# Units' lower parts are emitted one product later, and each MLP begins with a group of direct tiles, second-product tiles and 14 units

## The chip, the core and the metric

The kernel runs on one core of a Trainium2 chip. The core has five engines that run side by side and wait for each other through semaphores: TensorE (PE) multiplies matrices, VectorE (DVE), ScalarE (ACT) and GpSimd (POOL) work element by element, and SyncE (SP) issues the DMAs that bring weights from HBM. The on-chip memories are SBUF (operands) and PSUM (where TensorE accumulates). The metric is the device time of one launch in microseconds.

## The reference, cut to what matters

A trunk of two layers over 528 tokens (16 learned ones and 512 of the input), model width 1024. Layer 0 mixes with retention and gated DeltaNet heads, layer 1 with a Mamba-2 mixer. Each mixer is followed by a layernorm and by an MLP, and it is the two MLPs that the change touches:

```python
def sq_relu_mlp(h, w1, w2):
    return jnp.square(jax.nn.relu(h @ w1)) @ w2

for i in range(DEPTH):
    ...
    h = layer_norm(DN_ALPHA * h + mix, ln1_w[i], ln1_b[i])
    h = layer_norm(DN_ALPHA * h + sq_relu_mlp(h, mlp_w1[i], mlp_w2[i]), ln2_w[i], ln2_b[i])
return h[:, N_META:]
```

`w1` is 1024 x 4096 and `w2` 4096 x 1024, all in float32.

## The kernel before

**Precision.** A float32 product is made of three matmuls on split operands: high times high, high times low, low times high (`mm3`, L176 to L178). Every operand is therefore split once: ScalarE casts it to the high part (L152), VectorE subtracts to get the low part (L153). `halve` does this to a 1024-wide weight block, whose tiles are named `w`; activations split so are named `s`, and `hh` and `hl` are the halves of the normalised input of the MLP.

**Shape of the MLP.** `mlp()` is called for layer 0 and for layer 1. The tokens stand in the matmul's columns, in two halves: 272 and 256 in layer 0, 256 and 256 in layer 1, which drops the 16 learned tokens. Half a unit's columns are `nh`, 264 or 256. The hidden width of 4096 is 8 groups of 4 tiles of 128. A tile of the first product is 8 steps of 3 matmuls; in layer 1 some products run over 512 columns at once.

**Direct tiles.** `phase` (L191) runs tiles of the first product one after the other. The result is read from PSUM by `evac_u` (L445): ScalarE takes the Relu (L451), GpSimd squares it (L453), ScalarE squares it again into the rounded high part (L459), and VectorE subtracts the high part from GpSimd's square to get the low part (L460). High and low part are then the operands of the second product.

**Units.** From the second half of group 1 on, tiles come in pairs (`Unit`), as a Strassen-Winograd product: tiles i and i + 2 of a group, both halves of their rows and both halves of the tokens, in seven products of 12 matmuls (L514) instead of eight. `prepare` loads the weights, forms the sums s1 to s4 of weight quarters on VectorE (L487 s1, L488 s3, L490 s2, L491 s4) and splits all of them. `combos` makes the matching differences of the input (L408). `run` takes the products in the order a11, s1, s2, a12, s3, s4, a22. Three PSUM banks are used: `ba` for a11, s2, s3 and at last a22, `bb` for a12, `bc_` for s1 and s4. ScalarE copies intermediate sums out (L518, L521, L524) into the three rows x1, x2, x3, and VectorE adds to them: x1 += `bb` (L527), x2 += `ba` (L531), x3 += `bc_` (L535). The a22 product goes on writing into `ba`, so it has to wait until L531 has read it. Each of x1, x2, x3 and the final `ba` goes through `evac_u`.

**Second product.** `Four` takes four output tiles of `w2` for one group (96 matmuls in layer 0, 48 of 512 columns in layer 1) and adds them to the residual (`accumulate`: L385 the first time, L383 afterwards). It reads the high and low parts of all four tiles of its group.

**What sets the order.** The program is written as a list of `stages`; while one stage runs, `adv()` is called after each of its products and moves the preparation of the next stage on by one step, and `tick()` does the same for other spawned work such as `combos`. A scheduler fixes the order of the instructions of each engine when the kernel is built. Each engine then runs its instructions strictly in that order: an instruction that waits holds up everything behind it on its engine. Before the change, an MLP runs group 0 and tiles 0 and 2 of group 1 directly, then `unit(1, 1)`, `four(0, 0)`, `four(0, 1)`, and then in turn a unit of group c and a `Four` of group c - 1: 13 units per MLP.

Of the kernel before, what the change touches and what calls it, by code (L numbers as in the profile page):

```python
# [12 lines left out]
F32 = mybir.dt.float32  # L13
# [3 lines left out]
ADD, SUB, MUL, MIN, MAX, POW = ALU.add, ALU.subtract, ALU.mult, ALU.min, ALU.max, ALU.pow  # L17
# [40 lines left out]
def trunk(ctx: ExitStack, tc: tile.TileContext, a, out):  # L58
    nc = tc.nc
    V, G, S, T, SY = nc.vector, nc.gpsimd, nc.scalar, nc.tensor, nc.sync  # L60
# [37 lines left out]
    def spawn(gen):  # L98
        tasks.append(gen)
        return gen  # L100
# [18 lines left out]
    def wait(cond):  # L119
        while not cond():  # L120
            yield

    def until(cond):
        while not cond():
            tick()
# [14 lines left out]
    def pause(n):  # L140
        for _ in range(n):
            yield
# [29 lines left out]
    def wload(src, n=1024, raw=None):  # L172
        return halve(fetch(src, n) if raw is None else raw, n)
# [17 lines left out]
    def phase(tiles, rhs, evac, ns, head=0, tail=0, ready=None):  # L191

        def both(blks, key):
            o = pm(512)
            product(o, blks, rhs[2], every=4)
            for hf in range(2):
                evac(key, hf, o[:, hf * 256:hf * 256 + 256])
            tick()  # L200

        def run(hf, blks, key, m=P):
            o = pm(ns[hf], part=m)
            product(o, blks, rhs[hf], m=m)
            evac(key, hf, o)
            tick()
        n = len(tiles)
        for i0, i1 in [(0, head)] + [(i, i + 1) for i in range(head, n - tail)] + [(n - tail, n)]:
            held = []
            for srcs, *key in tiles[i0:i1]:  # L210
                held.append(([b for s in srcs for b in (s if isinstance(s, list) else s() if callable(s) else wload(s))], *key))
                if len(rhs) > 2 and head <= i0 < n - tail:
                    both(*held.pop())
                    continue
                if ready is not None and i0 == 0:
                    until(lambda: ready(0))
                run(0, *held[-1])
            if ready is not None and i0 == 0:
                until(lambda: ready(1))
            for args in held:  # L220
                run(1, *args)
# [20 lines left out]
    hx = [htile() for _ in range(KT)]  # L242
# [148 lines left out]
    def combos(h, ns, nh, go, get):  # L391

        def quarter(k, c):

            a, b = h[0][k], h[1][k]
            if c == 0:
                return [(0, nh, a[:, 0:nh])]
            cut = ns[0] - nh
            return ([(0, cut, a[:, nh:ns[0]])] if cut else []) + [(cut, nh, b)]

        def diff(out, x, y):
            if not isinstance(y, list):
                y = [(0, nh, y)]
            for o, e, ap in x:
                for o2, e2, ap2 in y:
                    lo, hi = max(o, o2), min(e, e2)
                    if lo < hi:
                        V.tensor_tensor(out[:, lo:hi], ap[:, lo - o:hi - o], ap2[:, lo - o2:hi - o2], op=SUB)  # L408

        yield from wait(go)  # L410
        for k in range(4):
            q0, q1 = [[quarter(i, c) for c in range(2)] for i in (k, k + 4)]
            d = [tl("m", nh) for _ in range(4)]
            diff(d[0], q0[1], q0[0])
            diff(d[2], q1[1], q0[1])
            diff(d[1], q1[1], d[0])
            diff(d[3], q1[0], d[1])
            for j in range(4):
                get(j, k, d[j])
                if j % 2:  # L420
                    yield

    def mlp(l, hx, h, ns, ready, evac0, pairs, final=None):
# [3 lines left out]
        w1, w2 = a["mw1"], a["mw2"]  # L427
        nh = (ns[0] + ns[1]) // 2
        NG, GF = 8, 4
        tt = [[None] * 4 for _ in range(4)]  # L430
# [7 lines left out]
        def half(k, i):  # L438
            return tuple(x[:, i * nh:(i + 1) * nh] for x in pairs[k])

        def group():
            u = [[None] * GF for _ in hx]
            us = [None] * GF

            def evac_u(f, hf, o, n=None):  # L445
                if n is None:
                    n, off = ns[hf], hf * ns[0]
                else:
                    off = hf * n
                t = tl("m", n)  # L450
                S.activation(t, o, AF.Relu)  # L451
                q = tl("m", n)
                G.tensor_tensor(q, t, t, op=MUL)  # L453
                if us[f] is None:
                    us[f] = pair = tl("s", L, F32R), tl("s", L, F32R)
                    for dst, x in zip(u, parts(pair, ((0, ns[0]), (ns[0], ns[1]), (0, 512)))):
                        dst[f] = x
                hi, lo = [x[:, off:off + n] for x in us[f]]
                S.activation(hi, t, AF.Square)  # L459
                V.tensor_tensor(lo, q, hi.bitcast(F32), op=SUB)  # L460
            return u, evac_u

        def second_src(c, m):
# [123 lines left out]

        groups = [group() for _ in range(NG)]

        def unit(c, i):  # L590
            return Unit(c, i, lambda f, hf, o: groups[c][1](f, hf, o, nh))

        def four(c, i):
            return Four(c, groups[c][0], 4 * i)

        stages = [unit(1, 1), four(0, 0), four(0, 1)]
        for c in range(2, NG):
            stages += [unit(c, 0), four(c - 1, 0), unit(c, 1), four(c - 1, 1)]
        last = [four(NG - 1, 0), four(NG - 1, 1)] if final is None else [Rows()]
        gens = [st.gen for st in stages + last]  # L600
        spawn(combos(h, ns, nh, lambda: ready(1), get))
        ahead = []

        def third():
# [3 lines left out]

        phase([([w1[l, 0]], 0), ([w1[l, 1]], 1), ([third], 2), ([lambda: halve(ahead[0])], 3)], hx, groups[0][1], ns,
              head=3, ready=ready)  # L610
        spawn(gens[0])

        def second():
            blks = wload(w1[l, GF + 2])
            next(gens[1])
            return blks

        phase([([w1[l, GF]], 0), ([second], 2)], hx, groups[1][1], ns)
        until(lambda: "s4" in stages[0].ops and all(x is not None for y in tt for x in y))
        B += [[half(k, 0) for k in range(4)], [half(k, 0) for k in range(4, 8)],  # L620
              [half(k, 1) for k in range(4, 8)], tt[3], tt[0], tt[1], tt[2]]
        for i, st in enumerate(stages):
            if i + 2 < len(gens):
                next(gens[i + 2])

            def adv():
                next(gens[i + 1], None)
                tick()
            st.run(adv)
            for _ in gens[i + 1]:  # L630
                pass
        for _ in gens[-1]:
            pass
        if final is not None:
            final(groups[-1][0][2], last[0].blks, h)
            return
        blks = last[0].blks + last[1].blks
# [511 lines left out]
    y = [[None] * 16, [None] * 16]  # L1149
# [21 lines left out]
    hn, hp, ready = norm_after(r, ns0, PP_LN, PP_LN + 8)  # L1171
# [3 lines left out]
    hn, hx, ready1 = norm_after(r, ns0, PP_LN + 16, PP_LN + 24)  # L1175
# [203 lines left out]
    for g in range(4):  # L1379
        f = []  # L1380
# [20 lines left out]
    for m in range(3):  # L1401
        blks = wload(srcs[m][0]) + wload(srcs[m][1][:, 0:512], 512)
        o = pm(512)
# [173 lines left out]
```

## Time and profile before

| | us |
|---|---|
| median of three runs | 1718.58 |
| the three runs | 1712.72, 1718.58, 1718.89 |
| profiled execution, its time | 1710.59 |
| profiled execution, its span in the trace | 1708.8 |
| busy: PE, DVE, ACT, POOL | 1662.7, 1154.1, 739.0, 316.9 |

The span is the time that the trace covers; the 1.8 us beside it lie around it. The mean granted clock of TensorE is 0.994 of full speed. PE is counted busy in 97% of the span, but matmuls are pipelined and their ends are modelled, so the start of one matmul to the start of the next is the better measure. The units of layer 0 run between about 575 and 872 us of the span, those of layer 1 between about 1380 and 1665 us. In a row of the trace the line is that of the kernel's text, tile names stand without their numbers, and `pmm` and `pmx` are PSUM tiles.

### The profile page before, as it was taken

The page shows a single profiled execution, that of the slowest core. Times are in us where ns is not written, and L with a number is a line of the kernel's source. Part 1 is how long each engine was busy: PE and PEld are TensorE (multiplying, and loading weights), DVE is VectorE, ACT ScalarE, POOL GpSimd, SP SyncE. Part 2 cuts the span into 40 slices and gives each one's busy share as a digit, 9 for nine tenths or more (in the row PEclk, how much of TensorE's full clock was granted, in tenths as well). Part 3 has the DMA queues.
Part 4 walks back from the last instruction along what each step waited for, and adds up shares of the span by engine and source line. Part 5 has one row for each costly group of instructions (what it writes and reads, how often), then busy time and mean ns, then how long its engine had stood idle before and what let it go on. Part 6 is the DMA issues. An engine that isn't in the chain of part 4 may idle for free.

```text
span 1708.8 us, 29912 instructions
## 1 busy us (share of the span) xinstructions
PE 1662.7 (97%) x11884; PEld 1529.0 (89%) x11884; DVE 1154.1 (68%) x2300; ACT 739.0 (43%) x1509; POOL 316.9 (19%) x360
## 2 busy tenths in 40 slices
PE   9899999999999999999999999999999999999998
PEld 7898998899999999999998988888778888888886
DVE  5896667666437857766657776858553876666665
ACT  4432245554214534444434665656432544444441
POOL 1211210010003301111102034242410321111112
PEclk9999999999999999999999999999999999999999
DMA  6233212112222322222221443333222222222231
GB/s 219 83 95 93 70 38 69 50 51 79 95 75 69 106 93 96 81 97 99 88 71 63 139 117 110 108 111 112 68 86 96 79 99 93 98 94 96 92 116 49
DMA packets 88484, 155.60 MB, mean 91 GB/s; under 512 B 11864, under 2 KB 43224, under 8 KB 88344
## 3 DMA queue, kind: packets, MB, share of 16 engines
q1 hardware_dynamic: 88200, 153.53, 28.1%
q8 instruction: 93, 1.52, 0.4%
q14 instruction: 47, 0.39, 0.1%
q10 hardware_dynamic: 144, 0.16, 0.0%
HBM read 148.92 MB, written 4.75 MB: 90 GB/s over the span
## 4 chain that ended last, share of the span: by engine, by line
PE 81%; DVE 8%; ACT 3%; POOL 3%; issue 2%; DMA 2%; SPq 0%; POOLq 0%; DVEq 0%; ACTq 0%
PE pmm L178 19%; PE pmm L177 19%; PE pmm L176 19%; PE pmm L514 7%; PE pmx L514 4%; POOL m L453 2%; ACT w L152 1%; DVE w L153 1%; PE pmx L1439 1%; DVE s L650 1%; DMA w<-in_w 1%; PE pmx L1289 1%; ACT m L451 1%; DVE s L460 1%; PE pmx L1293 1%
## 5 line engine op out<-in xcount | busy, mean ns | idle before, releaser
L176 PE MATMUL pmm<-hh,w 128*128 128x256 f32 (+5 forms) x1480 | 455.2, 308 | 5.6 <-ACT s L643 2.0
L178 PE MATMUL pmm<-hh,w 128*128 128x256 f32 (+3 forms) x1480 | 443.4, 300 | 0.2 <-DVE w L153 0.2
L177 PE MATMUL pmm<-hl,w 128*128 128x256 f32 (+3 forms) x1480 | 442.0, 299 | 1.2 <-DVE hl L344 0.9
L153 DVE TENSOR_TENSOR w<-w,w 128x1024 fp32r<-128x1024 f32 (+2 forms) x253 | 312.3, 1236 | 147.7 <-PE pmm L177 79.8
L152 ACT CAST w<-w 128x1024 fp32r<-128x1024 f32 (+2 forms) x253 | 260.9, 1032 | 347.5 <-PE pmm L177 88.9
L176 PE MATMUL pmm<-s,w 128*128 128x256 f32 (+2 forms) x1136 | 361.2, 318 | 0.0
L178 PE MATMUL pmm<-s,w 128*128 128x256 f32 (+2 forms) x1136 | 360.8, 318 | 0.0
L177 PE MATMUL pmm<-s,w 128*128 128x256 f32 (+2 forms) x1136 | 360.3, 317 | 0.0
L176 PEld LDWEIGHTS pmm<-hh,w 128*128 128x128 f32 (+2 forms) x1480 | 279.0, 189 | 19.5 <-issue 4.2
L177 PEld LDWEIGHTS pmm<-hl,w 128*128 128x128 f32 (+1 forms) x1480 | 278.8, 188 | 12.5 <-issue 2.1
L178 PEld LDWEIGHTS pmm<-hh,w 128*128 128x128 f32 (+1 forms) x1480 | 279.0, 189 | 8.8 <-DVE w L153 0.7
L177 PEld LDWEIGHTS pmm<-s,w 128*128 128x128 f32 x1136 | 213.7, 188 | 14.3 <-DVE s L1368 0.3
L176 PEld LDWEIGHTS pmm<-s,w 128*128 128x128 f32 x1136 | 213.9, 188 | 14.0
L178 PEld LDWEIGHTS pmm<-s,w 128*128 128x128 f32 x1136 | 213.7, 188 | 14.1
L453 POOL TENSOR_TENSOR m<-m 128x256 f32<-128x256 f32 (+2 forms) x128 | 117.1, 917 | 534.3 <-ACT m L451 530.8
L147 POOL TENSOR_TENSOR n<-n,neg 128x1 f32<-128x1 f32 (+2 forms) x58 | 40.3, 699 | 439.3 <-DVE n L146 418.7
L650 DVE SCALAR_TENSOR_TENSOR s<-s,pp,s 128x528 f32<-128x528 f32 x120 | 102.2, 851 | 27.1 <-ACT s L648 24.9
L383 DVE TENSOR_TENSOR m<-m,pmm 128x272 f32<-128x272 f32 (+1 forms) x208 | 81.7, 415 | 19.1 <-PE pmm L178 19.0
L460 DVE TENSOR_TENSOR s<-m,s 128x256 fp32r<-128x256 f32 (+2 forms) x128 | 64.9, 508 | 43.9 <-POOL m L453 41.5
L514 PE MATMUL pmm<-s,s 128*128 128x264 f32 (+1 forms) x624 | 83.8, 283 | 0.1
L514 PEld LDWEIGHTS pmm<-s,s 128*128 128x128 f32 x624 | 78.5, 188 | 0.5 <-DVE s L153 0.3
L527 DVE TENSOR_TENSOR row<-row,pmx 128x264 f32<-128x264 f32 (+1 forms) x26 | 11.0, 424 | 97.2 <-PE pmx L514 97.2
(313 smaller groups left out, 2464.8 us busy)
## 6 DMA issues: line engine op xcount, KB each, us to landing
w<-in_w SPq DMA_DIRECT2D x88, 512.0 KB, 3.2
w<-in_mw SPq DMA_DIRECT2D x146, 256.0 KB, 3.1
w<-in_mw SPq DMA_DIRECT2D x38, 512.0 KB, 3.3
w<-in_wo SPq DMA_DIRECT2D x29, 512.0 KB, 3.3
row<-rd SPq DMA_DIRECT2D x16, 512.0 KB, 5.6
sp<-in_mw SPq DMA_DIRECT2D x26, 256.0 KB, 2.7
s<-rd SPq DMA_DIRECT2D x32, 128.0 KB, 5.8
w<-in_w2n SPq DMA_DIRECT2D x4, 512.0 KB, 3.2
```

What stands on the lines that cost most here:

```text
L147: G.tensor_tensor(dst, t, neg5[0:part, 0:n], op=POW)
L152: S.copy(dst_hi, src)
L153: V.tensor_tensor(dst_lo, src, dst_hi.bitcast(F32), op=SUB)
L176: T.matmul(o, w[0], x[0], start=first, stop=False)
L177: T.matmul(o, w[0], x[1], start=False, stop=False)
L178: T.matmul(o, w[1], x[0], start=False, stop=last)
L383: V.tensor_tensor(t, t, o, op=ADD)
L451: S.activation(t, o, AF.Relu)
L453: G.tensor_tensor(q, t, t, op=MUL)
L460: V.tensor_tensor(lo, q, hi.bitcast(F32), op=SUB)
L514: T.matmul(o, w[x][:, c], B[b][k][y], start=first and k == i == 0, stop=last and k == 3 and i == 2, skip_group_check=True)
L650: V.scalar_tensor_tensor(acc, cin[:, k:k + L], w[k], acc, op0=MUL, op1=ADD)
```

## The change

Two things are done in `mlp()`.

First, the subtraction that makes the low part (L460) is no longer emitted in `evac_u` when a unit calls it. It is put on the list `late`, and `lower()`, called at the beginning of each `adv()`, emits those that were listed one product earlier. (In the changed file these subtractions have the line L598, those of direct tiles L462; a unit's additions are L531, L535 and L539 for L527, L531 and L535, its matmuls L518 for L514, and L487 to L491 become L491 to L495.)

Second, tiles 0 and 2 of group 1 are no longer direct tiles. Behind group 0 comes at once `four(0, 0)`, then `unit(1, 0)`, `four(0, 1)`, `unit(1, 1)`, and then the old sequence: 14 units per MLP. The weights of `four(0, 0)` are loaded and split during group 0 (`begin`), and `combos` starts one step later.

```diff
@@ combos
         yield from wait(go)
+        yield
         for k in range(4):
@@ group
-            def evac_u(f, hf, o, n=None):
+            def evac_u(f, hf, o, n=None, late=None):
...
                 S.activation(hi, t, AF.Square)
-                V.tensor_tensor(lo, q, hi.bitcast(F32), op=SUB)
+                if late is None:
+                    V.tensor_tensor(lo, q, hi.bitcast(F32), op=SUB)
+                else:
+                    late[-1].append((lo, q, hi.bitcast(F32)))
@@ mlp
+        late = [[], []]
+
+        def lower():
+            for lo, q, hi in late.pop(0):
+                V.tensor_tensor(lo, q, hi, op=SUB)
+            late.append([])
+
         def unit(c, i):
-            return Unit(c, i, lambda f, hf, o: groups[c][1](f, hf, o, nh))
+            return Unit(c, i, lambda f, hf, o: groups[c][1](f, hf, o, nh, late))
...
-        stages = [unit(1, 1), four(0, 0), four(0, 1)]
+        def begin():
+            yield from wait(lambda: ready(1))
+            yield from pause(2)
+            yield from gens[0]
+
+        stages = [four(0, 0), unit(1, 0), four(0, 1), unit(1, 1)]
         for c in range(2, NG):
             stages += [unit(c, 0), four(c - 1, 0), unit(c, 1), four(c - 1, 1)]
...
         spawn(combos(h, ns, nh, lambda: ready(1), get))
+        spawn(begin())
...
-        spawn(gens[0])
-
-        def second():
-            blks = wload(w1[l, GF + 2])
-            next(gens[1])
-            return blks
-
-        phase([([w1[l, GF]], 0), ([second], 2)], hx, groups[1][1], ns)
-        until(lambda: "s4" in stages[0].ops and all(x is not None for y in tt for x in y))
+
+        until(lambda: len(stages[0].blks) == 4 and all(x is not None for y in tt for x in y))
...
+        next(gens[1])
         for i, st in enumerate(stages):
             if i + 2 < len(gens):
                 next(gens[i + 2])
 
             def adv():
+                lower()
                 next(gens[i + 1], None)
                 tick()
             st.run(adv)
...
         for _ in gens[-1]:
             pass
+        lower()
+        lower()
```

VectorE around the additions of one unit in the middle of layer 0's MLP, before. The `row` tile holds x1, x2 and x3; `w` 128x1024 is a weight block being split, `s` 128x264 a low part:

```order
L527 TENSOR_TENSOR row_7822<-row_7822,pmx_7820 128x264
L153 TENSOR_TENSOR w_8003<-w_7813,w_8002 128x1024
L460 TENSOR_TENSOR s_7888<-m_7885,s_7887 128x264
L531 TENSOR_TENSOR row_7822<-row_7822,pmm_7819 128x264
L535 TENSOR_TENSOR row_7822<-row_7822,pmx_7821 128x264
L460 TENSOR_TENSOR s_7909<-m_7906,s_7908 128x264
```

and in the changed kernel, around the same unit:

```order
L531 TENSOR_TENSOR row_7835<-row_7835,pmx_7833 128x264
L153 TENSOR_TENSOR w_8016<-w_7826,w_8015 128x1024
L535 TENSOR_TENSOR row_7835<-row_7835,pmm_7832 128x264
L539 TENSOR_TENSOR row_7835<-row_7835,pmx_7834 128x264
L598 TENSOR_TENSOR s_7901<-m_7898,s_7900 128x264
L598 TENSOR_TENSOR s_7921<-m_7918,s_7920 128x264
```

The low part has left its place between the weight block and the x2 addition; now it stands behind the x3 addition, and the weight block is directly ahead of the x2 addition.

TensorE at the end of the same unit before, where `pmx` with `hh` is the last of product s4, `pmm` with 128x272 the following `Four` and `pmm` with 128x264 the product a22:

```order
L514 MATMUL pmx_7821<-hl_6448,s_7795 128x264
L514 MATMUL pmx_7821<-hh_6447,s_7796 128x264
L176 MATMUL pmm_7955<-s_6987,w_7836 128x272
L514 MATMUL pmm_7819<-s_6678,w_7741 128x264 x2
L514 MATMUL pmm_7819<-s_6678,w_7742 128x264
```

and in the changed kernel:

```order
L518 MATMUL pmx_7834<-hl_6448,s_7808 128x264
L518 MATMUL pmx_7834<-hh_6447,s_7809 128x264
L518 MATMUL pmm_7832<-s_6719,w_7754 128x264 x2
L518 MATMUL pmm_7832<-s_6719,w_7755 128x264
L518 MATMUL pmm_7832<-s_6814,w_7754 128x264 x2
```

The first matmul of the `Four` no longer stands ahead of a22.

VectorE ahead of the first unit's additions in layer 0, before, with the preparation of the next unit (L487, L488, L490) between them:

```order
L460 TENSOR_TENSOR s_7073<-m_7105,s_7072 128x256
L153 TENSOR_TENSOR s_7126<-s_7028,s_7125 128x512
L487 TENSOR_TENSOR w_7267<-sp_7268,w_7267 128x512
L527 TENSOR_TENSOR row_7138<-row_7138,pmx_7136 128x264
L488 TENSOR_TENSOR sp_7268<-w_7265,sp_7268 128x512
L153 TENSOR_TENSOR w_7286<-w_7129,w_7285 128x1024
L460 TENSOR_TENSOR s_7204<-m_7201,s_7203 128x264
L531 TENSOR_TENSOR row_7138<-row_7138,pmm_7135 128x264
L490 TENSOR_TENSOR sp_7268<-w_7267,w_7265 128x512
L535 TENSOR_TENSOR row_7138<-row_7138,pmx_7137 128x264
```

and in the changed kernel, where the first unit is `unit(1, 0)` and two units' preparations (`w` and `sp` tiles of two numbers) stand around its additions:

```order
L385 SCALAR_TENSOR_TENSOR m_5896<-m_5896,pmm_7101 128x256
L153 TENSOR_TENSOR w_7156<-w_6975,w_7155 128x1024
L491 TENSOR_TENSOR w_7117<-sp_7118,w_7117 128x512
L492 TENSOR_TENSOR sp_7118<-w_7115,sp_7118 128x512
L494 TENSOR_TENSOR sp_7118<-w_7117,w_7115 128x512
L491 TENSOR_TENSOR w_7252<-sp_7253,w_7252 128x512
L531 TENSOR_TENSOR row_7124<-row_7124,pmx_7122 128x264
L492 TENSOR_TENSOR sp_7253<-w_7250,sp_7253 128x512
L535 TENSOR_TENSOR row_7124<-row_7124,pmm_7121 128x264
L153 TENSOR_TENSOR w_7305<-w_7115,w_7304 128x1024
L598 TENSOR_TENSOR s_7190<-m_7187,s_7189 128x264
L539 TENSOR_TENSOR row_7124<-row_7124,pmx_7123 128x264
```

A second preparation, L491 to L494, has come in ahead of the L491 whose place is before the first addition; L598 stands behind the second addition.

TensorE behind the last tile of group 0 in layer 0 (its second half ends in the first row), before:

```order
L178 MATMUL pmm_6915<-hh_6447,w_6862 128x256
L176 MATMUL pmm_6958<-hh_6384,w_6954 128x272
L177 MATMUL pmm_6958<-hl_6385,w_6954 128x272
L178 MATMUL pmm_6958<-hh_6384,w_6955 128x272
L176 MATMUL pmm_6958<-hh_6393,w_6954 128x272
L177 MATMUL pmm_6958<-hl_6394,w_6954 128x272
```

Tile 0 of group 1 followed, with the normalised input `hh` and `hl`. In the changed kernel:

```order
L178 MATMUL pmm_6912<-hh_6447,w_6870 128x256
L176 MATMUL pmm_6978<-s_6562,w_6776 128x272
L177 MATMUL pmm_6978<-s_6563,w_6776 128x272
L178 MATMUL pmm_6978<-s_6562,w_6777 128x272
L176 MATMUL pmm_6978<-s_6654,w_6776 128x272
L177 MATMUL pmm_6978<-s_6655,w_6776 128x272
L178 MATMUL pmm_6978<-s_6654,w_6777 128x272
L176 MATMUL pmm_6978<-s_6712,w_6776 128x272
L177 MATMUL pmm_6978<-s_6713,w_6776 128x272
L178 MATMUL pmm_6978<-s_6712,w_6777 128x272
L176 MATMUL pmm_6978<-s_6902,w_6776 128x272
L176 MATMUL pmm_6995<-s_6562,w_6776 128x256
```

Now the second product follows, with the squared activations `s`. Its fourth operand, `s_6902`, is made from the tile that ends in the first row, and it comes after nine matmuls.

## The prediction

> **What bounds the kernel now.** The first view is the page's chain of work that ended last; the second is the list of groups by line and shape, which keeps the matmuls of the two MLPs apart (264 wide in layer 0, 256 wide in layer 1).
>
> ```profile
> PE 81%; DVE 8%; ACT 3%; POOL 3%; issue 2%; DMA 2%; SPq 0%; POOLq 0%; DVEq 0%; ACTq 0%
> ...
> L514 PE MATMUL pmm<-s,w 128*128 128x264 f32 x156 | 22.6, 294 | 8.4 <-DVE row L531 8.4
> ...
> L514 PE MATMUL pmm<-s,w 128*128 128x256 f32 x156 | 21.9, 289 | 6.1 <-DVE row L531 6.1
> ```
>
> TensorE carries 81% of the chain, so time falls only where it has less to do or waits less. The two L514 rows are the a22 products of the 26 units (156 = 13 x 12 matmuls): 14.5 us of TensorE's idle time stand in front of them, all released by the addition in L531. The timeline of one unit in layer 0 shows why. Its columns are start, duration, engine, line, operation, and in brackets the idle time before it with its releaser.
>
> ```profile
> 616.73 1.63 PE L514 MATMUL pmm<-s,s 128*128 128x264 f32 x12
> 617.00 0.43 DVE L527 TENSOR_TENSOR row<-row,pmx 128x264 f32<-128x264 f32 x1 [4.41 <-PE pmx L514]
> 617.89 1.22 DVE L153 TENSOR_TENSOR w<-w,w 128x1024 fp32r<-128x1024 f32 x1 [0.46 <-ACT w L152]
> 618.19 0.28 PE L514 MATMUL pmx<-hh,s 128*128 128x264 f32 x1
> 618.25 1.34 POOL L453 TENSOR_TENSOR m<-m 128x264 f32<-128x264 f32 x1 [27.75 <-ACT m L451]
> 619.63 0.43 DVE L460 TENSOR_TENSOR s<-m,s 128x264 fp32r<-128x264 f32 x1 [0.52 <-POOL m L453]
> 619.65 0.29 PE L176 MATMUL pmm<-s,w 128*128 128x272 f32 x1
> 619.98 0.42 DVE L531 TENSOR_TENSOR row<-row,pmm 128x264 f32<-128x264 f32 x1
> 620.46 1.74 PE L514 MATMUL pmm<-s,w 128*128 128x264 f32 x12 [0.52 <-DVE row L531]
> ```
>
> VectorE's addition L531 has had its data since product s3 ended at about 618.2, but the lower part L460 is queued ahead of it and waits for GpSimd's square, which ends at 619.59. TensorE starts one matmul of the next stage at 619.65 and would go on to a22 0.13 us later, at 619.78; it does so at 620.46. **Lost: 0.68 us.** The same stretch in layer 1:
>
> ```profile
> 1386.23 1.57 PE L514 MATMUL pmm<-s,s 128*128 128x256 f32 x12
> 1387.40 1.23 DVE L153 TENSOR_TENSOR w<-w,w 128x1024 fp32r<-128x1024 f32 x1
> 1387.64 0.28 PE L514 MATMUL pmx<-hh,s 128*128 128x256 f32 x1
> 1387.93 1.16 POOL L453 TENSOR_TENSOR m<-m 128x256 f32<-128x256 f32 x1 [5.36 <-ACT m L451]
> 1389.06 0.40 PE L176 MATMUL pmm<-s,w 128*128 128x512 f32 x1
> 1389.13 0.42 DVE L460 TENSOR_TENSOR s<-m,s 128x256 fp32r<-128x256 f32 x1 [0.51 <-POOL m L453]
> 1389.47 0.41 DVE L531 TENSOR_TENSOR row<-row,pmm 128x256 f32<-128x256 f32 x1
> 1389.94 1.67 PE L514 MATMUL pmm<-s,w 128*128 128x256 f32 x12 [0.48 <-DVE row L531]
> 1391.44 0.39 PE L177 MATMUL pmm<-s,w 128*128 128x512 f32 x1
> ...
> 1392.61 0.39 PE L176 MATMUL pmm<-s,w 128*128 128x512 f32 x1
> ```
>
> Five 512-wide matmuls lie between the last two rows, so their pace is 1.17 / 5 = 0.234 us; a22 should have started at 1389.06 + 0.23 = 1389.29 and started at 1389.94. **Lost: 0.65 us.**
>
> **The change, part by part.** *The wait.* With the lower part emitted one product later, VectorE has the x1 addition, the 1024-wide cast (L153), the x2 addition. Layer 0: the cast ends at 617.89 + 1.22 = 619.11, the addition 0.42 later at 619.53, and a22, now directly behind s4, is due at 619.65. From addition to matmul the rows show 620.46 - (619.98 + 0.42) = 0.06 us, so the addition releases a22 at 619.59: 0.06 early. Layer 1: 1387.40 + 1.23 + 0.41 + 0.06 = 1389.10 against 1389.06: 0.04 late, or just in time, since successive VectorE starts overlap by about 0.08 (L460 to L531 above: 0.35 apart, 0.43 long). So the wait goes, and **the cast is next in line with almost nothing to spare**. The bounds are nothing gained and all gained; I take all but 0.02 a unit: 12 x 0.68 + 13 x 0.65 = 16.6, less 0.5, gives **-16.1 us** (each layer has 13 units; the first of layer 0 is priced below). The delayed subtractions are needed only a stage later, by the next second product (over 10 us of matmuls), which hides them. If that cover were gone, each 0.43 us would be TensorE's again.
>
> *The units.* Four direct products (two tiles, two halves) become seven of 12 matmuls in each MLP. In layer 0, 24 matmuls each of 272 and of 256 columns take 3.02 and 2.85 us by these starts:
>
> ```profile
> 563.19 0.29 PE L176 MATMUL pmm<-hh,w 128*128 128x272 f32 x1
> ...
> 566.21 0.28 PE L176 MATMUL pmm<-hh,w 128*128 128x256 f32 x1
> ...
> 569.06 0.29 PE L176 MATMUL pmm<-hh,w 128*128 128x272 f32 x1
> ```
>
> Two of each are 11.7 us; seven products at 618.19 - 616.73 = 1.46 are 10.2. In layer 1, 48 x 0.234 = 11.2 against 7 x (1387.64 - 1386.23 = 1.41) = 9.9. Together **-2.8 us**. VectorE gets 20 instructions more (0.4 to 1.2 us each, some 12 us), ScalarE 12; both have idle time beside 81% TensorE, and if that cover is gone it is in the starts, below.
>
> *The first unit.* It now has a second product ahead of it. Before, its additions stood behind L487, the preparation of the next unit, which waited for weights:
>
> ```profile
> 582.10 0.69 DVE L487 TENSOR_TENSOR w<-sp,w 128x512 f32<-128x512 f32 x1 [2.74 <-DMA w<-in_mw]
> ...
> 586.21 1.00 PE L514 MATMUL pmm<-s,w 128*128 128x264 f32 x6 [2.09 <-DVE row L531]
> ```
>
> In the new order two such L487s stand ahead of its additions, and their loads are issued after casts on VectorE. Bounds: gone (-2.1), or the 2.74 us wait met once more with a second load behind it (+2.7). I take half of the gain, **-1.0**.
>
> *The starts of the two MLPs.* TensorE waits for the layernorm there, and its clock then halves. Windows; columns are busy time of PE, PEld, DVE, ACT, POOL with the count, granted clock, DMA share, GB/s:
>
> ```profile
> 547.20:550.60 3.40, 2.01 (x14) 1.61 (x14) 3.40 (x10) 1.73 (x5) 0.56 (x1) 1.00 0.16 30
> 550.60:554.00 3.40, 3.40 (x19) 3.40 (x18) 2.87 (x9) 2.37 (x6) 1.35 (x2) 0.50 0.32 127
> 554.00:557.40 3.40, 3.40 (x30) 3.40 (x30) 2.89 (x9) 2.41 (x8) 1.75 (x2) 1.00 0.43 149
> 1352.70:1356.10 3.40, 2.02 (x12) 1.42 (x12) 3.40 (x11) 1.31 (x4) 0.11 (x1) 1.00 0.03 5
> 1356.10:1359.50 3.40, 3.40 (x17) 3.40 (x17) 2.89 (x8) 2.45 (x7) 1.68 (x2) 0.50 0.41 154
> ```
>
> Idle are 1.39 and 1.38 us; at half clock 11 and 13 matmuls fewer than in the 30 of a full window, at 0.12 us, so 1.3 and 1.6 us. In the new program TensorE's order alternates matmuls of tiles 0 and 1 while the second half's operands come in, which can fill part of the wait; but the work waited for is VectorE's (3.40 busy of 3.40), and it now has a cast of the second product's weights in front. Bounds: 0 and -5.7 for both MLPs; I take half, -2.8.
>
> Against this, the second product starts right behind tile 3 and needs tile 3's squared output as its fourth operand, after 9 matmuls. What that takes when VectorE is full shows in the rows of layer 1 below; the first row is an undisturbed square of GpSimd in layer 0, for comparison:
>
> ```profile
> 623.02 0.63 POOL L453 TENSOR_TENSOR m<-m 128x264 f32<-128x264 f32 x1 [0.45 <-ACT m L451]
> ...
> 1368.54 0.39 PE L178 MATMUL pmm<-hh,w 128*128 128x512 f32 x1
> 1369.53 0.38 ACT L451 ACTIVATE m<-pmm 128x256 f32<-128x256 f32 x1
> 1369.98 3.52 POOL L453 TENSOR_TENSOR m<-m 128x256 f32<-128x256 f32 x2 [2.27 <-ACT m L451]
> 1372.96 1.16 DVE L460 TENSOR_TENSOR s<-m,s 128x256 fp32r<-128x256 f32 x2 [0.51 <-POOL m L453]
> ```
>
> From 1368.8 to 1374.1 it is 5.3 us; 9 matmuls of 0.234 cover 2.1, so a wait of 3.2 us is the upper bound and none the lower. GpSimd there took 3.5 us for two squares, beside casts that the new order has elsewhere; with two squares of 0.63 us the chain is 2.2 us shorter and the wait 1.0. I take 1.3 us per MLP for what VectorE has queued, near the lower end: +2.6. **The starts: -0.2.**
>
> Here a page can be weighed. Behind both windows with 1.4 us of idle time the clock is 0.50. The Trainium skill, "TensorE: Matmul & The Clock Gate", Part 1, lets the clock fall only after a whole idle window of about 3.4 us. These windows were 59% busy and were followed by 0.50, so the trace does not bear it out. By that rule the halved stretches have another cause and stay: the sum would be 1.5 us smaller.
>
> **Sum:** -16.1 - 2.8 - 1.0 - 0.2 = **-20.1 us**, which takes the profiled execution from 1710.6 to 1690.5. The runs shown are 1712.7, 1718.6 and 1718.9; the mean of the four is 1715.2, and from this I forecast **1695**.
>
> **The rivals.**
> *A: GpSimd holds the addition up.* The x2 addition now falls beside GpSimd's square, and VectorE operations beside one can take twice as long:
>
> ```profile
> 623.05 0.89 DVE L460 TENSOR_TENSOR s<-m,s 128x264 fp32r<-128x264 f32 x1
> ...
> 1024.13 2.03 POOL L1302 TENSOR_TENSOR s<-s,s 128x512 f32<-128x512 f32 x1
> 1025.18 0.41 DVE L1326 SCALAR_TENSOR_TENSOR s<-m,pmm 128x256 f32<-128x256 f32 x1
> ```
>
> This L460 starts beside the square of 623.02 quoted above, reads two SBUF tiles and is held; L1326 reads one from PSUM, as the addition does, and takes its usual 0.41 inside a GpSimd operation. Were the addition held to the square's end: 619.59 + 0.48 = 620.07 in layer 0 (0.42 still lost, 0.26 gained), 1389.09 + 0.47 = 1389.56 in layer 1 (0.50 lost, 0.15 gained); 12 x 0.26 + 13 x 0.15 = 5.1, and the sum -9.1: **1706**. Chance 0.13.
>
> *B: the starts eat the gain.* Both new waits at 3.2 us, the old idle time and half clock kept, the first unit's wait kept: -16.1 - 2.8 + 6.4 = -12.5, **1703**. For it speaks that VectorE is full there; against it that the costly GpSimd squares came from casts. Chance 0.11.
>
> *C: the clock rule.* The halved stretches stay: **1697**. Chance 0.05.
>
> *D: slower.* Late weights in every unit: if L487 to L490 of the next unit, which VectorE runs ahead of the x1 addition, waited for their load as they did at 582.10, each wait would pass to TensorE. VectorE stands idle 4.41 us before the x1 addition in the row of 617.00, so weights must land 4.41 us later before anything is lost, and 20.1 / 28 units = 0.72 us beyond that before the kernel is slower than now; with one wait of 2.09 in each of 28 units it is -20.1 + 58.5, **1754**. The loads' order within a unit is the same, which speaks against it. Chance 0.02.
>
> *E: no effect.* If the subtraction were scheduled back ahead of the addition, only the units' 2.8 us remain: **1712**. The printed order has it behind both additions. Chance 0.01.
>
> **How the numbers follow.** The forecast has the rest, 0.68. The range: the full start gains and no new wait (-20.1 - 2.9 - 2.6 - 1.1 = -26.7) from the fastest separate run give 1686; A and B with the spread of the slower runs give 1710. About 0.5% is what a measurement of this kernel can tell from no change, 1710 to 1727 around the median: of the forecast, A, B and C some 0.86 lie below 1710, D and unlucky starts make 0.04 above 1727, and 0.10 is between.
>
> **What would show it.** The L514 rows for a22 (L518 in the changed file) should lose their 8.4 and 6.1 us of idle time, with the cast L153 as the last to end before the addition; if A holds, the addition lasts 0.8 us instead of 0.42. At each MLP's start, look for TensorE's wait on the lower part of tile 3, and for windows at clock 0.50. The forecast fails if the cast itself comes later (it waits for ScalarE's cast, which waits for product a12), for then every unit keeps a wait of that size.

## The result and the profile after

| | before | changed |
|---|---|---|
| median, us | 1715.65 (4 runs) | 1691.45 (4 runs) |
| lowest and highest, us | 1709.34, 1718.89 | 1690.39, 1694.62 |
| ratio of the runs | | 0.9866, 95% interval 0.9831 to 0.9902 |
| profiled execution: its time, span | 1710.59, 1708.8 | 1694.62, 1692.8 |

The changed kernel is 24 us faster by the medians; 20.1 were forecast, and its median is 4 us under the forecast of 1695, inside the range. In a second comparison its median was 1692.03 against 1715.36 (ratio 0.9868, 0.9850 to 0.9886).

First the groups by line and shape. The a22 products, 14 units in each layer now, answer to the two rows of before that had 8.4 and 6.1 us of idle time:

```profile
L518 PE MATMUL pmm<-s,w 128*128 128x256 f32 x168 | 22.8, 285 | 0.0
L518 PE MATMUL pmm<-s,w 128*128 128x264 f32 x168 | 22.8, 285 | 0.0
```

No idle time is left. The timeline of one unit in layer 0 shows the new order:

```profile
636.43 1.63 PE L518 MATMUL pmm<-s,s 128*128 128x264 f32 x12
...
636.70 0.43 DVE L531 TENSOR_TENSOR row<-row,pmx 128x264 f32<-128x264 f32 x1 [4.43 <-PE pmx L518]
...
637.60 1.22 DVE L153 TENSOR_TENSOR w<-w,w 128x1024 fp32r<-128x1024 f32 x1 [0.47 <-ACT w L152]
...
638.03 1.28 POOL L454 TENSOR_TENSOR m<-m 128x264 f32<-128x264 f32 x1 [17.34 <-ACT m L452]
...
638.74 0.42 DVE L535 TENSOR_TENSOR row<-row,pmm 128x264 f32<-128x264 f32 x1
...
639.36 1.62 PE L518 MATMUL pmm<-s,w 128*128 128x264 f32 x12
...
639.90 1.06 DVE L598 TENSOR_TENSOR s<-m,s 128x264 fp32r<-128x264 f32 x2
```

The x2 addition (L535) follows the low part of the weight block (L153 on VectorE, which the prediction calls the cast) and ends at 639.16, 0.20 us before a22 starts; the two lower parts (L598) come behind. GpSimd's square runs from 638.03 to 639.31, so the addition lies wholly beside it and still takes 0.42: nothing holds it. In layer 1 the same four instructions are closer together:

```profile
1454.53 1.23 DVE L153 TENSOR_TENSOR w<-w,w 128x1024 fp32r<-128x1024 f32 x1 [0.47 <-ACT w L152]
...
1454.95 1.27 POOL L454 TENSOR_TENSOR m<-m 128x256 f32<-128x256 f32 x1 [16.75 <-ACT m L452]
...
1455.67 0.41 DVE L535 TENSOR_TENSOR row<-row,pmm 128x256 f32<-128x256 f32 x1
...
1456.20 1.65 PE L518 MATMUL pmm<-s,w 128*128 128x256 f32 x12
```

Here 0.12 us are left, of which 0.06 is the way to TensorE. From one unit to the next unit (first matmul to first matmul, ten periods each) it is 22.71 us before and 21.93 after in layer 0, 21.81 and 21.15 in layer 1.

At the starts of the MLPs the two waits of before behind the layernorm (0.47 and 0.91 us in layer 0, 0.48 and 0.89 in layer 1) are gone; smaller ones stand earlier, the longest 0.61 us ahead of a matmul of the layernorm (L334) in layer 0 and 0.35 us in layer 1. New ones stand where `four(0, 0)` needs tile 3. Layer 0:

```profile
561.85 0.39 ACT L452 ACTIVATE m<-pmm 128x272 f32<-128x272 f32 x1
...
562.32 1.88 POOL L454 TENSOR_TENSOR m<-m 128x272 f32<-128x272 f32 x2 [3.36 <-ACT m L452]
...
562.75 0.51 PE L176 MATMUL pmm<-s,w 128*128 128x272 f32 x2 [1.20 <-ACT s L460]
...
563.66 1.17 DVE L462 TENSOR_TENSOR s<-m,s 128x272 fp32r<-128x272 f32 x2 [0.53 <-POOL m L454]
...
564.55 0.40 PE L177 MATMUL pmm<-s,w 128*128 128x272 f32 x1 [1.29 <-DVE s L462]
...
1363.70 0.50 PE L176 MATMUL pmm<-s,w 128*128 128x512 f32 x1 [0.85 <-ACT s L460]
...
1365.41 0.50 PE L177 MATMUL pmm<-s,w 128*128 128x512 f32 x1 [1.21 <-DVE s L462]
```

The last two rows are layer 1. TensorE waits first for the high part, then for the low part: 2.49 us in layer 0, 2.06 in layer 1.

Where the time went is read from landmarks: the first matmul of each of the three layernorm groups that frame the MLPs (L334), and the end of the last matmul.

| stretch, us | before | changed |
|---|---|---|
| layernorm and MLP of layer 0 (524.9 to 908.6; 524.6 to 897.1) | 383.7 | 372.5 |
| layer 1's mixer (to 1332.2; to 1327.4), not touched | 423.6 | 430.3 |
| layernorm and MLP of layer 1 (to 1701.2; to 1685.1) | 369.0 | 357.7 |

The two MLPs give 22.5 us. The mixer runs the same code in both, so its 6.7 us more are put down to the executions: the second one of the changed program that was profiled has 426.9 there with one clock window (3.4 us) at half clock, this one has three such windows, and the one of before has none. In the other profiled kernels, whose mixer is the same too, it takes 425.3 to 430.9. For this reason the two spans differ by 16 us only, and the medians by 24.

### The profile page after: what moved, and what is told of

It reads as the page before. It is cut to its first block, busy times and chain, and to the rows that moved or that the text cites. A ratio compares the mean times of both kernels' runs of the same rounds, so it can differ in the third digit from the quotient of the medians.

```text
span 1692.8 us, 29970 instructions
## 1 busy us (share of the span) xinstructions
PE 1657.8 (98%) x11908; PEld 1531.4 (90%) x11908; DVE 1169.0 (69%) x2320; ACT 746.6 (44%) x1521; POOL 313.4 (19%) x360
## 4 chain that ended last, share of the span: by engine, by line
PE 86%; DVE 6%; DMA 2%; ACT 2%; issue 2%; POOL 1%; SPq 0%; POOLq 0%; DVEq 0%; ACTq 0%
PE pmm L176 19%; PE pmm L178 19%; PE pmm L177 19%; PE pmm L518 10%; PE pmx L518 7%; DMA w<-in_w 2%; DVE s L664 1%; PE pmx L1453 1%; DVE w L153 1%; PE pmx L274 1%; PE pmx L334 1%; PE pmx L1303 1%; PE pmx L1307 1%; POOL n L147 1%; PE pmx L995 1%
## 5 line engine op out<-in xcount | busy, mean ns | idle before, releaser
L176 PE MATMUL pmm<-hh,w 128*128 128x256 f32 (+6 forms) x1432 | 438.5, 307 | 3.9 <-ACT s L657 2.6
L178 PE MATMUL pmm<-hh,w 128*128 128x256 f32 (+6 forms) x1432 | 427.5, 299 | 0.4 <-DVE w L153 0.4
L177 PE MATMUL pmm<-hl,w 128*128 128x256 f32 (+6 forms) x1432 | 425.9, 298 | 0.8 <-POOL hl L344 0.4
L153 DVE TENSOR_TENSOR w<-w,w 128x1024 fp32r<-128x1024 f32 (+2 forms) x253 | 312.3, 1235 | 144.2 <-PE pmm L177 78.4
L176 PEld LDWEIGHTS pmm<-hh,w 128*128 128x128 f32 (+2 forms) x1432 | 269.0, 188 | 17.2 <-issue 4.2
L177 PEld LDWEIGHTS pmm<-hl,w 128*128 128x128 f32 (+2 forms) x1432 | 269.0, 188 | 10.8 <-issue 2.1
L178 PEld LDWEIGHTS pmm<-hh,w 128*128 128x128 f32 (+2 forms) x1432 | 269.2, 188 | 8.3 <-DVE w L153 0.9
L454 POOL TENSOR_TENSOR m<-m 128x256 f32<-128x256 f32 (+2 forms) x128 | 112.1, 879 | 517.1 <-ACT m L452 479.7
L518 PE MATMUL pmm<-s,s 128*128 128x264 f32 (+1 forms) x672 | 89.8, 282 | 0.0
L518 PEld LDWEIGHTS pmm<-s,s 128*128 128x128 f32 x672 | 84.5, 188 | 0.0
L531 DVE TENSOR_TENSOR row<-row,pmx 128x264 f32<-128x264 f32 (+1 forms) x28 | 11.9, 425 | 91.7 <-PE pmx L518 91.7
L598 DVE TENSOR_TENSOR s<-m,s 128x264 fp32r<-128x264 f32 (+1 forms) x112 | 66.5, 612 | 1.9 <-POOL m L454 1.3
```

The costliest lines, as they stand in the source:

```text
L153: V.tensor_tensor(dst_lo, src, dst_hi.bitcast(F32), op=SUB)
L176: T.matmul(o, w[0], x[0], start=first, stop=False)
L177: T.matmul(o, w[0], x[1], start=False, stop=False)
L178: T.matmul(o, w[1], x[0], start=False, stop=last)
L518: T.matmul(o, w[x][:, c], B[b][k][y], start=first and k == i == 0, stop=last and k == 3 and i == 2, skip_group_check=True)
L598: V.tensor_tensor(lo, q, hi, op=SUB)
```

## The experiments

Each ratio is to the kernel before, run in turn with it on the same chip.

**The two parts alone.** The later subtraction in the kernel before (old stages):

```diff
-                V.tensor_tensor(lo, q, hi.bitcast(F32), op=SUB)
+                if late is None:
+                    V.tensor_tensor(lo, q, hi.bitcast(F32), op=SUB)
+                else:
+                    late[-1].append((lo, q, hi.bitcast(F32)))
... (late, lower() and unit() as in the change)
             def adv():
+                lower()
```

> The kernel before with the lower parts one product later and nothing else (13 units per MLP, old start). Theory 1, the wait ahead of a22 is most of the gain: 25 units x 0.66 us go, and some 0.5 of the first unit's wait, so about 17 us less than before (ratio 0.990), and no idle time of TensorE ahead of a22 except in the first unit of layer 0. Rival, the new stages bring most of it (no halved clock at the starts, one unit more per MLP): 8 us less or under, ratio 0.995 or above.

And the changed kernel with the subtraction at once:

```diff
-            return Unit(c, i, lambda f, hf, o: groups[c][1](f, hf, o, nh, late))
+            return Unit(c, i, lambda f, hf, o: groups[c][1](f, hf, o, nh))
```

> The changed kernel with the subtraction emitted at once as before (14 units per MLP, new start). Theory 1: 28 units wait 0.66 us again, so about 18 us of the gain go and 3 to 6 us of it stay (ratio to before 0.997 to 0.998); idle time of about 0.5 us stands ahead of every a22. Rival: 12 us or more of the gain stay (ratio 0.993 or under).

Measured: the later subtraction alone 1693.86 against 1714.30, ratio 0.9882 (0.9863 to 0.9901); the new stages alone 1713.79 against 1714.30, ratio 0.9999 (0.9987 to 1.0012). The a22 groups of the first, and then of the second:

```profile
L517 PE MATMUL pmm<-s,w 128*128 128x264 f32 x156 | 21.3, 286 | 2.9 <-DVE row L534 2.9
...
L517 PE MATMUL pmm<-s,w 128*128 128x256 f32 x156 | 21.1, 284 | 0.0
```

```profile
L518 PE MATMUL pmm<-s,w 128*128 128x264 f32 x168 | 24.1, 293 | 7.0 <-DVE row L535 7.0
...
L518 PE MATMUL pmm<-s,w 128*128 128x256 f32 x168 | 23.6, 290 | 6.9 <-DVE row L535 6.9
```

In the first only one wait is left, 2.9 us, that of the first unit of layer 0; it was 2.09 before, so the half of it that was expected to go did not. In the second nearly every unit waits, 0.50 us in the mean of the 28. The 20.4 us of the first are more than the 17 expected, which its interval (17.0 to 23.5 us) just takes in. So the place of one 0.4 us instruction is some 20 of the 24 us, and the stages with 28 units, alone, are worth nothing that can be measured, though less than the 3 to 6 us expected.

**How near the next bound is.** One more addition on VectorE ahead of the x2 addition:

```diff
                 prod(ba, "s3", 6, False, False)
+                V.tensor_tensor(tl("m", nh), x1, bb, op=ADD)
                 V.tensor_tensor(x2, x2, ba, op=ADD)
```

> The changed kernel with one more addition of nh columns on VectorE (its result is not used) between the x1 and the x2 addition of every unit. In the profile after, the x2 addition ends 0.20 us (layer 0) and 0.12 us (layer 1) before a22 starts, of which 0.06 is the way from VectorE to TensorE. Theory, the cast is next in line with a margin of 0.14 and 0.06 us: the addition takes 0.34 us more of VectorE's line, 14 x 0.20 + 14 x 0.28 = 6.7 us more than the changed kernel (about 1698). Rival, the margin is larger than it looks because something else holds a22: 1 us or less.

Measured: 1697.80, ratio 0.9907 (0.9887 to 0.9928), 6 us over the changed kernel. The rows, where L535 is the addition that was added and L536 the x2 addition:

```profile
640.45 0.42 DVE L535 TENSOR_TENSOR m<-row,pmx 128x264 f32<-128x264 f32 x1
...
640.79 0.42 DVE L536 TENSOR_TENSOR row<-row,pmm 128x264 f32<-128x264 f32 x1
...
641.07 0.28 PE L176 MATMUL pmm<-s,w 128*128 128x272 f32 x1
641.27 0.39 PE L518 MATMUL pmm<-s,w 128*128 128x264 f32 x1
```

VectorE is 0.34 us later, and a22 starts at 641.27, 0.20 after its due time at 641.07, into which the scheduler has put a matmul of the next stage again. The delay of 0.20 is met in layer 0, but that matmul is work and not loss; the cost is better read from the periods, which grow by 0.18 us in layer 0 and only 0.11 in layer 1 (0.28 were expected), 4 us in 28 units. The 6 us of the runs are not precise enough to tell 4 from 6.7. The margin is real: about a third of one VectorE instruction.

**The waits at tile 3.** In the order of ScalarE's instructions casts of `combos` stand ahead of tile 3's Relu (the one of 561.85), so three other places for `combos` were tried: later by six steps, later by two, and one earlier, as in the kernel before.

```diff
         yield from wait(go)
-        yield
+        yield from pause(7)
```

> The changed kernel with combos begun six steps later (pause of 7 in place of one yield), so that the casts of combos stand behind tile 3's Relu and Square on ScalarE. Theory 2, the new waits at the starts (2.8 us in layer 0, 2.5 in layer 1, and a halved clock behind the first) come from ScalarE's Relu of tile 3 standing behind casts that wait for VectorE's differences: they shrink to 1 us or less each, 3 to 5 us less than the changed kernel. Rival, VectorE is full there and the work only moves: unit(1, 0) then waits for the differences, and the time is the same as the changed kernel's within 2 us, or longer.

Measured: 1707.03, ratio 0.9962 (0.9947 to 0.9976), 15 us over the changed kernel. At tile 3 little is left, but the first unit now waits for its operands:

```profile
571.96 0.39 PE L518 MATMUL pmx<-s,w 128*128 128x264 f32 x1 [1.72 <-ACT s L152]
...
574.91 1.53 PE L518 MATMUL pmx<-s,w 128*128 128x264 f32 x3 [1.72 <-ACT s L152]
577.37 0.58 PE L176 MATMUL pmm<-s,w 128*128 128x256 f32 x1 [0.92 <-DVE m L385]
```

The wait moved and grew, as the rival has it. With `pause(3)`:

> The changed kernel with combos begun two steps later than in it (pause of 3). Between the changed kernel (waits of 2.8 and 2.5 us at tile 3's operand) and the run with a pause of 7 (0.7 and 0.9 there, but about 7 us at unit(1, 0)): if the cost only moves, there is no better place and the time is 0 to 8 us above the changed kernel; if casts on ScalarE alone were the matter, 2 to 4 us below it.

Measured: 1694.94, ratio 0.9890 (0.9874 to 0.9906), 2.9 us over the changed kernel's 1692.03 of the same comparison, inside the 0 to 8 us expected where the cost only moves. And without the added step:

```diff
         yield from wait(go)
-        yield
```

> The changed kernel without the added yield ahead of combos, as in the kernel before. If the casts of combos ahead of tile 3's Relu cause the new waits, the waits at four(0, 0) grow, by up to 1 us per MLP, 0 to 2 us in all; rival, the yield does nothing that can be measured, within 0.5 us.

Measured: 1698.45, ratio 0.9909 (0.9893 to 0.9925), 6.4 us over it. That was neither expectation: the waits at tile 3 grew, but the old waits behind the layernorm were back too:

```profile
551.30 0.39 PE L177 MATMUL pmm<-hl,w 128*128 128x256 f32 x1 [0.49 <-DVE hl L344]
...
552.71 0.39 PE L176 MATMUL pmm<-hh,w 128*128 128x256 f32 x1 [0.90 <-ACT m L451]
```

These are the 0.47 and 0.91 us of the kernel before. So the added `yield`, which the prediction gave no term of its own, is what removes them here.

**Does the yield work by itself?** It was put into the kernel before, without and with the later subtraction:

> The kernel before with only the added yield ahead of combos (old stages, subtraction at once). In the changed kernel the yield was worth 6.4 us, and without it the two waits behind the layernorm (0.65 and 1.07 us in layer 0, nearly the same in layer 1) and the halved clock behind them were back. Theory 3, the yield works by itself: the same waits and halved stretches of the kernel before go, 5 to 6.5 us less than before (ratio 0.996 to 0.997). Rival, it needs the new start: within 1.5 us of before.

> The kernel before with the lower parts one product later and the added yield, but the old start and 13 units per MLP. If theory 3 holds, 20.4 + 5 to 6 us less than before, 1689 to 1691, no slower than the changed kernel (1692), and the new start with its 28 units adds nothing. Rival, the yield needs the new start: 1693 to 1695, as with the later subtraction alone.

Measured: 1713.36 against 1713.36, ratio 1.0003 (0.9990 to 1.0016), and 1694.67, ratio 0.9890 (0.9873 to 0.9908). Theory 3 fell, and both are as its rival has them. In the first of them the waits behind the layernorm are gone, and the first units wait instead:

```profile
578.55 3.01 PE L515 MATMUL pmm<-s,s 128*128 128x264 f32 x12 [2.83 <-ACT row L519]
```

```profile
1384.95 1.32 PE L515 MATMUL pmm<-s,s 128*128 128x256 f32 x6 [1.94 <-ACT row L519]
```

**Work for TensorE during the wait.** In `four(0, 0)` the operands of tiles 0 to 2 come first for four products in layer 0 and three in layer 1, and tile 3's at the end:

```diff
...
+                    for j in range(js[0]):
+                        for hf in ((2,) if wide else (0, 1)):
+                            o = px(512 if wide else ns[hf])
+                            product(o, [self.blks[j]], self.u[hf], k0=0, k1=3)
+                            part.append((j, hf, o))
+                    for j, hf, o in part:
+                        product(o, [self.blks[j]], self.u[hf], k0=3)
...
```

> The changed kernel once more, on the chip of the next three, as their base: 0.983 to 0.990 of before by its first runs, about 1691.

> The changed kernel with the first second-product stage written so that TensorE first does the three operands of tiles 0 to 2 for four products in layer 0 (36 matmuls, 4.4 us) and three in layer 1 (27 matmuls, 6.3 us), and then tile 3's operand for each; they use the other PSUM pool. Theory 2, TensorE merely lacks work while tile 3's operand is made: the waits of 2.8 and 2.5 us and the halved clock behind the first go, 4 to 7 us less than the changed kernel. Rival, VectorE bounds the start and unit(1, 0) waits for its operands instead: under 2 us.

Measured: the changed kernel 1692.03, this one 1690.75, ratio 0.9864 (0.9849 to 0.9879), against 0.9868 (0.9850 to 0.9886). The waits at tile 3 are gone; in their place, in layer 0:

```profile
572.02 0.50 PE L518 MATMUL pmx<-s,w 128*128 128x264 f32 x2 [0.74 <-ACT w L152]
573.97 0.52 PE L518 MATMUL pmx<-s,w 128*128 128x264 f32 x2 [1.45 <-DVE w L153]
```

and 1.61 us ahead of the first a22 of layer 1. The rival holds: the first unit waits instead, and the gain is under 2 us. Of the kernels that compute everything it has the lowest median, but it is not clear of the changed kernel.

**VectorE's work taken away, or moved.** Without the low parts of `combos`, and with them on GpSimd:

```diff
-            split(hl[:, 0:nh], hl[:, nh:2 * nh], x)
-            tt[j][k] = hl[:, 0:nh], hl[:, nh:2 * nh]
+            S.copy(hl[:, 0:nh], x)
+            tt[j][k] = hl[:, 0:nh], hl[:, 0:nh]
```

> The changed kernel without the 16 subtractions per MLP that make the low parts of combos' differences (VectorE, 0.35 us from start to start, 5.6 us per MLP); the matmuls read the high part twice instead, so the low part of the input's differences is left out. Theory 4, VectorE bounds the start of each MLP and every rearrangement only moves the wait: with 5.6 us less of its work the waits at tile 3's operand (2.8 and 2.5 us, and 1.2 behind L385 or a halved clock) shrink to under half without coming back at unit(1, 0), 3 to 7 us less than the changed kernel (1692). Rival, ScalarE's Relu behind the casts is the limit: the casts stay, so under 1.5 us.

```diff
-            split(hl[:, 0:nh], hl[:, nh:2 * nh], x)
+            S.copy(hl[:, 0:nh], x)
+            G.tensor_tensor(hl[:, nh:2 * nh], x, hl[:, 0:nh].bitcast(F32), op=SUB)
```

> The changed kernel with those 16 subtractions per MLP on GpSimd, which is idle there. If theory 4 holds and GpSimd does not disturb VectorE, 3 to 6 us less than the changed kernel; but VectorE operations that read two SBUF tiles were seen to wait for a running GpSimd operation (0.89 us in place of 0.43), and tile 3's squares stand in GpSimd's queue too: then the gain is under 1 us or the time is up to 4 us longer. I hold the second for likelier.

Measured: 1689.81, ratio 0.9860 (0.9842 to 0.9878), about 2 us under the changed kernel and not clear of it; and 1707.11, ratio 0.9959 (0.9945 to 0.9972), 15 us over it. Of the first:

```profile
564.05 0.39 PE L177 MATMUL pmm<-s,w 128*128 128x272 f32 x1 [1.38 <-DVE s L462]
...
565.93 0.38 PE L177 MATMUL pmm<-s,w 128*128 128x256 f32 x1 [0.18 <-DVE s L462]
```

The wait in layer 0 went from 2.49 to 1.38 + 0.18 = 1.56 us, with no halved stretch behind it, and did not come back at the first unit, but it did not halve. So VectorE's load is a part of it; the rest is the chain of Relu, square and subtraction behind a tile that has just ended. In that chain GpSimd's square is itself held up by VectorE. In the same run:

```profile
561.20 0.68 DVE L494 TENSOR_TENSOR sp<-w,w 128x512 f32<-128x512 f32 x1
...
561.42 2.10 POOL L454 TENSOR_TENSOR m<-m 128x272 f32<-128x272 f32 x1 [2.34 <-ACT m L452]
```

The square that the wait of 1.38 us hangs on takes 2.10 us there, beside this addition and a 1.22 us subtraction of VectorE behind it; undisturbed it takes 0.63 (the prediction's row of 623.02), and 2.10 - 0.63 is more than the whole wait. In the changed kernel it takes 1.31 us, and the first subtraction behind it 0.83 in place of 0.42, so by these rows an estimated 1.1 of the 2.49 us there (0.68 and 0.41) come of the two engines standing in each other's way. No run tests this by itself.

In the second run, GpSimd's subtractions slow VectorE down; the same five differences in the changed kernel and there:

```profile
565.52 1.24 DVE L408 TENSOR_TENSOR m<-m,m 128x256 f32<-128x256 f32 x5
```

```profile
563.94 2.20 DVE L408 TENSOR_TENSOR m<-m,m 128x256 f32<-128x256 f32 x5
...
563.95 0.87 POOL L455 TENSOR_TENSOR m<-m 128x256 f32<-128x256 f32 x1
564.88 0.91 POOL L437 TENSOR_TENSOR s<-m,s 128x264 fp32r<-128x264 f32 x1
```

In layer 0 tile 3's operands come this late:

```profile
567.40 0.39 PE L176 MATMUL pmm<-s,w 128*128 128x272 f32 x1 [2.70 <-ACT s L461]
570.50 0.60 PE L177 MATMUL pmm<-s,w 128*128 128x272 f32 x1 [2.71 <-DVE s L463]
```

With 1.95, 2.51 and 1.40 us of wait in layer 1, and five clock windows at half clock among and behind these waits where the changed kernel has one, most of the 15 us is accounted for. The expectation that VectorE would be held was right, and the loss was larger than the 4 us given. The Trainium skill, "SBUF — State Buffer", section "SBUF: two separate sides", says that GpSimd and a VectorE operation with two SBUF inputs take one pair of ports by an exclusive lock and that the loser is blocked for the whole instruction. These rows agree as far as they go: side by side VectorE's five take 2.20 us in place of 1.24 and GpSimd's two 0.87 and 0.91 in place of some 0.6. So does the x2 addition, which has one input in PSUM and was not held (0.42).

## Why the prediction was right, point by point

- **The wait ahead of a22.** Right in mechanism; the size was 2 us too small. The periods give 12 x 0.78 + 13 x 0.66 = 17.9 us for the -16.1 of the sum. What the rows of before did not count in layer 0 is the first matmul behind a wait: a22 took 1.74 us there and takes 1.62 now.
- **The cast is next in line.** Right, with the margins of the sum: 0.14 and 0.06 us after the 0.06 to TensorE, and the run with one more addition made it bind.
- **The first unit.** Wholly gone, 2.1 us by its row; half was taken. The later subtraction alone left it standing (2.9 us), so it is the new start that removes it.
- **The starts.** The net was right by luck (-0.2 forecast, about +0.3 measured): both of its halves were too small, and the errors cancel. The old waits went, for a reason that the prediction didn't have, the added `yield`. With the halved stretches behind them that is -5.7 us in the two profiled executions for the -2.8 taken, but the halved stretches belong to the execution as much as to the kernel: with the later subtraction alone the same waits stand (0.48 and 0.91, 0.48 and 0.89 us), each pair falls into two clock windows, with 2.77 and 2.64, 2.92 and 2.51 us of busy time, and none of these is followed by half clock. The new waits are 2.49 + 2.06 = 4.6 us for the 2.6 taken, and a halved stretch follows the first of them in the profiled execution. From the MLPs' 22.5 us less 17.9, 2.8 and 2.1 there remain 0.3 us that the starts cost.
- **The units' -2.8 us** have no run of their own, but the size of a unit can be read: two units follow each other directly in the new order, and from one a22 to the next it is 10.24 us in layer 0 and 10.00 in layer 1, for the 10.2 and 9.9 of the sum. The new stages alone give 0.9999, from 2.2 us faster to 2.1 slower. The units, the first unit's wait and three more units that wait 0.66 us each make -2.9 together, so the new start cost somewhat more than the old one in those runs, or one of these terms is smaller; which is not shown.
- **Rival A** fell by the 0.42 us of L535 beside a running square, **E** by the order of the rows, **D** by the idle time of VectorE ahead of L531, 4.43 us as before. **B** has the right place and about two thirds of its price for the new waits, but the old waits did not stay. **C** fell: no half clock follows the layernorm in the changed kernel, nor with the later subtraction alone, where its waits stand.

What stays open is how much of the waits at tile 3 could be had at all: the rearrangements here moved them, to the first unit or back to the layernorm, and the one run with less work on VectorE took some of them away. How much of the rest is GpSimd's square held up by VectorE is open too.

## What to carry to other kernels

An engine runs its queue in order, so look for an instruction that waits for a third engine ahead of one that the bottleneck waits for, and let the waiting one be emitted a step later: 0.4 us of work cost some 0.7 us in each of 25 units. Before counting on such a gain, work out what ends last after it, and how far away that is. Where an engine is full over a stretch, as VectorE is at these starts, a new order mostly moved the wait: count the engine's work there first.

## What the runs showed of the hardware

The same wait is followed by half clock in one execution and not in another. Windows of two executions of the changed program (columns as in the prediction), each with about 2.5 us of idle time ahead of tile 3's operand; the first has them in one window of the clock, in the second they fall into two:

```profile
561.70:565.10 3.40, 1.05 (x6) 0.84 (x7) 2.87 (x7) 2.27 (x7) 1.88 (x2) 1.00 0.00 0
565.10:568.50 3.40, 3.40 (x18) 3.40 (x18) 3.40 (x14) 1.52 (x4) 0.00 (x0) 0.50 0.00 0
```

```profile
561.10:564.50 3.40, 2.20 (x18) 1.98 (x18) 3.40 (x13) 1.75 (x5) 0.58 (x1) 1.00 0.00 0
564.50:567.90 3.40, 2.11 (x16) 1.90 (x17) 2.87 (x10) 1.44 (x5) 1.30 (x2) 1.00 0.00 0
567.90:571.30 3.40, 2.39 (x19) 2.17 (x18) 3.40 (x12) 1.18 (x4) 0.00 (x0) 1.00 0.00 0
```

Behind the window with 1.05 us of busy time the clock is 0.50; behind those with 2.20 and 2.11 us it stays at 1.00, though the idle time is nearly the same in sum (2.35 and 2.49 us). The time came out the same even so, since VectorE was behind: in the second execution TensorE, at full clock, then waited for it,

```profile
570.48 0.39 PE L176 MATMUL pmm<-s,w 128*128 128x256 f32 x1 [1.01 <-DVE m L385]
```

and from the layernorm (L334) to the fourth unit layer 0 took 105.97 us in the first execution and 105.88 in the second. The Trainium skill, "TensorE: Matmul & The Clock Gate", Part 1, calls the window free-running, with which this agrees; that it takes a whole idle window does not hold here, nor in the kernel before, where windows with 2.01 and 2.02 us of busy time (and 14 and 12 matmuls) were followed by 0.50. Nor does the busy time alone decide: in that same trace the window from 584.70, with 1.89 us and 15 matmuls, was followed by 1.00. Which windows are hit changes from execution to execution, and this is a part of the spread between runs of one program: of the changed kernel's four runs the longest (1694.62) has a mean granted clock of 0.992 and the shortest (1690.39) 0.995, and one window of 3.4 us at half clock takes 0.001 off it.
